# The heads' norms: squares summed in two f32r products in place of one fp32 product

## The chip, the cores and the metric

One core of a Trainium2 chip runs the whole kernel in one launch. TensorE (PE; its weight loads are shown as PEld), VectorE (DVE), ScalarE (ACT) and GpSimd (POOL) each work through a queue of their own in order, and wait for each other through semaphores; transfers are issued by SyncE (SP) and by POOL. The metric is the device time in microseconds (us) of one execution. Before the change it is 901.6 us, the median of three runs that lie between 899.93 and 905.34 us.

## The reference

One layer of a hybrid transformer on 528 tokens (16 meta tokens and 512 others) of width 1024, in fp32. Three kinds of attention run on the same normed input: stick-breaking heads (`sb`, 4 heads), sparse heads that see the 132 best keys by an indexer (`sp`, 4 heads), and differential heads (`df`, 4 heads, two maps each). Each has a gate and an output projection; then come `w_out`, a residual, and a gated feed-forward net with a short convolution. What the change touches is the norm over the channels of a head:

```python
def _rmsnorm(a, gain):
    af = a.astype(jnp.float32)
    af = af * lax.rsqrt(jnp.mean(af * af, axis=-1, keepdims=True) + EPS)
    return (af * gain.astype(jnp.float32)).astype(a.dtype)
...
    _indexed_sparse_attention(_rmsnorm(hd(q_sp, SP_HEADS), q_norm_sp),
                              _rmsnorm(hd(k_sp, SP_HEADS), k_norm_sp), ...)
    q_df = _rmsnorm(q_df.reshape(b, tp, DF_HEADS, 2, HEAD_DIM), q_norm_df)
    k_df = _rmsnorm(k_df.reshape(b, tp, DF_HEADS, 2, HEAD_DIM), k_norm_df)
    ...
    y_df = _rmsnorm(y_df, subln_df) * (1.0 - lam_init)
```

## The kernel before

Activations stand with channels on the 128 partitions and tokens along the row, so 128 channels (two heads of 64) of 528 tokens are one tile. Each dense product is made of three f32r products: an fp32 number is split into a rounded f32r part (`xh`, `wh`) and what is left (`xl`, `wl`), and hi*hi + lo*hi + hi*lo is summed in PSUM (`mm3`). A dense chunk of 128 outputs takes two halves of the tokens (258 and 256 columns, or 264 twice), and each half 24 products of TensorE into a bank `psd`; DVE then multiplies the bank by the row norm `rs` into SBUF. These last steps are the evacuations.

The work from 100 us on follows a list, `PLAN`: units (`sb0`, `df0`, ..., `sp1`: a q, a k and a v chunk each), gate chunks (`g0a`, ...) and branch projections (`b0a`, ...). The piece of the list that matters here is `... df3 g2b sp0 sp1 b2a b2b g1a g1b b1a b1b`. Beside this main line run streams, Python generators that are advanced one step after every eight dense products (`tick`): for each unit one for q, k and v (norm, split, moves between partitions), one for the scores and weights, one for the products with the values, and for `df` one for the output `y`. The top-132 search of the indexer (`topk_stream`) is another stream: 17 rounds of `max` and `match_replace` on DVE over four blocks of queries, one round per `PACE` of the planner's clock. The `sp` scores wait until it is finished (`picked`).

When a stream goes on is decided while the program is built, by booked costs: every DVE, ACT and POOL instruction adds a cost to a clock of its engine (`book`), every product to PE's (`pe`; `mm` books an fp32 product of n columns at 2*0.844*n ns and an f32r product at 0.46*n+1 ns), and `settle` holds a stream until PE's clock has passed what it waits for. So a change of costs moves other instructions as well. A branch cannot start before the outputs of its units are booked as done (`until`): `b2a` needs `y` of all four `df` units, and its TensorE instructions stand behind them in PE's queue.

`headnorm` is the step that is changed. It is used for q and k of `sp0`, `sp1` and `df0` to `df3` (12 norms, constant `blk`: two blocks of 64x64 with -0.5/64) and for the output of `df0` to `df3` (4 norms, constant `ones2` with -0.5/128). ACT squares the tile, TensorE multiplies the square with the constant in two halves, which leaves in every partition the sum over the head's channels, and `rstd` makes 1/sqrt of it (Ln, Exp, Square on ACT, two steps on DVE). 16 norms of two halves are 32 products; a product of fp32 operands shows in the trace as two MATMUL records with two weight loads. In the trace `ones2` is called `ones`, and all instructions of the three vector engines have line 99, that of the booking helper.

Of the kernel before, what the change touches and what calls it, by code (L numbers as in the profile page):

```python
# [8 lines left out]
F32 = mybir.dt.float32  # L9
F32R = mybir.dt.float32r  # L10
AF = mybir.ActivationFunctionType
OP = mybir.AluOpType
# [3 lines left out]
P = 128  # L16
# [39 lines left out]
def tile_kernel(ctx: ExitStack, tc, hT, wpk, par, bias, yT):  # L56
# [25 lines left out]
    class Timed:  # L82
# [11 lines left out]
        def __getattr__(self, op):  # L94
            f = getattr(self.eng, op)

            def run(out, *a, **k):
# [5 lines left out]
    V = Timed("V", nc.vector, 1.04, 150, scalar_tensor_tensor=(1.25, 105), tensor_tensor_scan=(2.16, 110),  # L103
              tensor_tensor_reduce=(1.0, 255), match_replace=(1.04, 220))
    S = Timed("S", nc.scalar, 0.84, 190)
# [18 lines left out]
    def pe(cost):  # L124
        c = cur[0]
        ready = c["t"] if c["t"] != c.get("pe") and c is not main else 0
        clock["P"] = max(clock["P"], ready) + cost
        c["t"] = c["pe"] = clock["P"] + LAT


    const = ctx.enter_context(tc.tile_pool(name="const", bufs=1))
# [12 lines left out]
    def bank(tag):  # L144

        while sum(h["t"] + BSL > clock["P"] for h in held[tag]) >= banks[tag]:
            yield
        h = {"t": math.inf}
        held[tag].append(h)
        return ps.tile([P, 512], F32, tag=tag, bufs=banks[tag], name="ps" + tag), h  # L150

    def drop(h):
        h["t"] = cur[0]["t"]
# [9 lines left out]
    def give(tag, n=1):  # L163
        free[tag] += n
        assert free[tag] <= caps[tag], tag
# [5 lines left out]
    def wait(tag, n=1):  # L171
        while free[tag] < n:
            yield
        take(tag, n)

    def tmp(dt=F32):
        return ap_.tile([P, T], dt, tag="tmp", bufs=caps["tmp"], name="tmp")

    def mm(out, lhsT, rhs, **k):

        n, w = rhs.shape[-1], 0.84 * max(32, lhsT.shape[-1])
        pe(max(0.46 * n + 1, w) if rhs.dtype == F32R else 2 * max(0.844 * n, w))
        PE.matmul(out, lhsT, rhs, **k)  # L183
# [38 lines left out]
    def settle(more=0):  # L222

        c = cur[0]
        while clock["P"] < c["t"] + more + SLACK:
            yield
# [23 lines left out]
    make_identity(nc, ident)  # L250
    onesd = const.tile([P, P], F32, name="onesd")
    V.memset(onesd, -0.5 / D)
    ones2 = const.tile([P, P], F32, name="ones2")
    V.memset(ones2, -0.5 / 128)
    blk = const.tile([P, P], F32, name="blk")
    V.memset(blk, 0.0)
    V.memset(blk[0:64, 0:64], -0.5 / 64)
    V.memset(blk[64:128, 64:128], -0.5 / 64)
    eps = const.tile([P, 1], F32, name="eps")
    V.memset(eps, EPS)  # L260
    one = const.tile([P, 1], F32, name="one")
# [18 lines left out]
    for w in plan:  # L280
# [5 lines left out]
        else:  # L286
            n = BRW[br] // 2
# [97 lines left out]
    def wbank():  # L385
        return ps.tile([P, 512], F32, tag="w", bufs=banks["w"], name="psw")
# [21 lines left out]
    ixd, st = [wbank(), wbank()], [wbank(), wbank()]  # L408
# [16 lines left out]
    def rstd(dst, st, y0, a, now=True):  # L425

        S.activation(dst, st, AF.Ln, bias=eps, scale=-2.0)
        S.activation(y0, dst, AF.Exp, scale=-0.5)
        S.activation(a, y0, AF.Square)
        rstd2(dst, st, y0, a) if now else None  # L430

    def rstd2(dst, st, y0, a):
        V.scalar_tensor_tensor(a, st, -0.5 * EPS, a, OP.add, OP.mult)
        V.scalar_tensor_tensor(dst, a, 1.5, y0, OP.add, OP.mult)

    y0, a0 = tmp(), tmp()
# [199 lines left out]
    def headnorm(raw, n, gain, mat):  # L636

        yield from wait("tmp", 4)
        sq, r, y0, a = tmp(), tmp(), tmp(), tmp()
        S.activation(sq[:, :n], raw[:, :n], AF.Square)  # L640
        yield from settle()
        for o, w in (HALQ if n == TQ else HALF):
            t0 = cur[0]["t"]
            st, b = yield from bank("w")
            cur[0]["t"] = 0
            mm(st[:, :w], mat, sq[:, o:o + w], start=True, stop=True)
            x = r[:, o:o + w], st[:, :w], y0[:, o:o + w], a[:, o:o + w]
            rstd(*x, now=False)
            yield from settle(-SET)
            rstd2(*x)  # L650
            drop(b)
            yield
        V.scalar_tensor_tensor(raw[:, :n], raw[:, :n], gain, r[:, :n], OP.mult, OP.mult)
        give("tmp", 4)
# [7 lines left out]
    def q_stream(unit, raw, gain):  # L662


        n = TQ
        if gain is not None:
            yield from headnorm(raw, n, gain, blk)
        yield from wait("qk", 2)
        yield from wait("tmp")
        a, b, l = qtile(), qtile(), tmp(F32R)  # L670
        S.copy(a[:, :n], raw[:, :n])
        sub(l[:, :n], raw[:, :n], a[:, :n])
        move(b[64:128, :n], a[64:128, :n])
        move(b[0:64, :n], l[64:128, :n])
        move(a[64:128, :n], l[0:64, :n])
        give("tmp", 2)
        unit["q"] = (a, b)
        unit["t"] = max(unit.get("t", 0), cur[0]["t"] + 6500)

    def k_stream(unit, raw, gain):  # L680


        n = T
        if gain is not None:
            yield from headnorm(raw, n, gain, blk)
        yield from wait("qk", 4)
        a, b, l, m = qtile(), qtile(), qtile(), qtile()
        S.copy(a, raw)
        sub(l, raw, a)
        for x, y in ((a, b), (l, m)):  # L690
            move(y[64:128], x[64:128])
            move(y[0:64], x[64:128])
            move(x[64:128], x[0:64])
        give("tmp")
        unit["k"] = (a, b, l, m)
        unit["t"] = max(unit.get("t", 0), cur[0]["t"] + 6500)
# [286 lines left out]
    def y_stream(unit, paired):  # L983
        yr = unit["yr"]
        if not paired:
            yield from headnorm(yr, TQ, gsub, ones2)
        yield from wait("y", 2)
        yh, yl = (ap_.tile([P, TQ], F32R, tag="y", bufs=caps["y"], name="y") for _ in range(2))
        S.copy(yh, yr[:, :TQ])
        sub(yl, yr[:, :TQ], yh)  # L990
        give("tmp")
        unit["y"] = (yh, yl)
        unit["done"] = cur[0]["t"]
# [92 lines left out]
    for m in range(8):  # L1086
        a = gates[0, m // 4][:, m % 4]
# [12 lines left out]
    def ft(dt=F32):  # L1100
        return ffn.tile([P, TQ], dt, tag="ft", bufs=10, name="ft")

    for m in range(8):
# [18 lines left out]
        sq = ss if m == 0 else ft()  # L1122
# [36 lines left out]
    for f in range(NF):  # L1159
# [11 lines left out]
        a = ft()  # L1171
# [9 lines left out]
    for m in range(8):  # L1181
# [3 lines left out]
        for c in sorted({e // 8 for e in range(e0, e1)}):  # L1185
# [5 lines left out]
                start=es[0] == e0, stop=es[-1] == e1 - 1)  # L1191
# [77 lines left out]
```

## Time and profile before

| | us |
|---|---|
| median of three runs | 901.6 |
| the profiled execution | 906.82 |
| its span on the core | 904.7 |
| PE busy in the span | 869.8 |
| DVE busy | 534.1 |
| ACT busy | 453.6 |
| POOL busy | 248.9 |

The span is the time from the first to the last instruction of the core in the trace, and the 2.1 us around it are launch and end. A share of the whole span is an average over stages: the start to about 100 us, the attention with its dense chunks to about 360 us, the branches and the last units to about 480 us, and the output projection and the feed-forward net to the end. Rows of a timeline give the start (us from the span's start), the duration, the engine, the line, the operation, the tiles out<-in and the count of merged instructions.

### The profile page before, as it was taken

To read this page: it belongs to the slowest core of one execution; us is meant where nothing else is said; L and a number is where in the kernel's file an instruction comes from. 1 tells how busy PE (TensorE), PEld (TensorE's weight loads), DVE (VectorE), ACT (ScalarE), POOL (GpSimd) and SP (SyncE) were. 2 spreads that over 40 slices of the span, in tenths; PEclk is the share of its full clock that TensorE was granted. 3 is DMA by queue.
4 is the path that set the end of the run, shared out by engine and by line. 5 is a ranking of instruction groups with operands and counts; after the bars stand their busy time and mean duration, and the time that the engine had idled before them with its cause. 6 is when DMAs were issued, how large, how long until landed. Compare 5 with 4: busy or idle time off the path is not lost.

```text
span 904.7 us, 15408 instructions
## 1 busy us (share of the span) xinstructions
PE 869.8 (96%) x6066; PEld 808.5 (89%) x6066; DVE 534.1 (59%) x1145; ACT 453.6 (50%) x848; POOL 248.9 (28%) x200
## 2 busy tenths in 40 slices
PE   6898999999999999699998999999999999999998
PEld 6897999999999999698998999999999999888886
DVE  6559969888778787777446444455444444322221
ACT  6446877787757777554663353333333333211110
POOL 2335012131113112564043234444434444200100
PEclk9899999999999999899999999999999999999999
DMA  6576635574557644643554323323333233333330
GB/s 210 161 199 195 159 92 132 136 164 107 111 126 174 153 116 113 146 97 81 130 117 161 95 76 93 93 93 94 93 96 92 93 94 96 97 118 110 117 108 29
DMA packets 35959, 107.79 MB, mean 119 GB/s; under 512 B 4713, under 2 KB 4857, under 8 KB 35888
## 3 DMA queue, kind: packets, MB, share of 16 engines
q1 hardware_dynamic: 27968, 78.19, 28.9%
q0 software_dynamic: 7920, 28.64, 15.0%
q8 instruction: 47, 0.77, 0.4%
q14 instruction: 24, 0.20, 0.1%
HBM read 93.99 MB, written 5.86 MB: 110 GB/s over the span
## 4 chain that ended last, share of the span: by engine, by line
PE 76%; DVE 10%; ACT 4%; DMA 4%; POOL 2%; issue 2%; SPq 0%; ACTq 0%; POOLq 0%; DVEq 0%
PE psd L183 53%; PE psw L183 21%; DVE tmp L99 4%; ACT tmp L99 2%; PE psw L187 2%; DMA wr<-wpk 2%; DMA qk<-qk 1%; DVE work L99 1%; DVE G L99 1%; ACT wl L99 1%; POOL tmp L99 1%; DVE wl L99 1%; DMA wh<-wpk 1%; DVE m L99 1%; DMA wl<-wpk 1%
## 5 line engine op out<-in xcount | busy, mean ns | idle before, releaser
L99 ACT CAST wh<-wr 128x1024 fp32r<-128x1024 f32 (+2 forms) x112 | 114.2, 1021 | 219.3 <-DMA wr<-wpk 171.9
L99 DVE TENSOR_TENSOR wl<-wr,wh 128x1024 fp32r<-128x1024 f32 (+2 forms) x80 | 93.2, 1166 | 70.1 <-PE psd L183 67.9
L99 POOL TENSOR_TENSOR wl<-wr,wh 128x1024 fp32r<-128x1024 f32 x32 | 81.1, 2537 | 180.1 <-PE psd L183 95.0
L183 PE MATMUL psd<-xh,wh 128*128 128x258 f32 (+2 forms) x792 | 119.5, 290 | 5.1 <-DVE tmp L99 3.5
L183 PE MATMUL psd<-xh,wl 128*128 128x258 f32 (+2 forms) x792 | 117.0, 288 | 1.1 <-POOL wl L99 1.1
L183 PE MATMUL psd<-xl,wh 128*128 128x258 f32 (+2 forms) x792 | 117.7, 289 | 0.0
L183 PEld LDWEIGHTS psd<-xh,wh 128*128 128x128 f32 x792 | 105.0, 191 | 6.9 <-issue 3.6
L183 PEld LDWEIGHTS psd<-xh,wl 128*128 128x128 f32 x792 | 104.1, 191 | 2.1 <-POOL wl L99 1.3
L183 PEld LDWEIGHTS psd<-xl,wh 128*128 128x128 f32 x792 | 104.4, 190 | 0.7
L99 ACT ACTIVATE tmp<-tmp 128x528 f32<-128x528 f32 (+7 forms) x154 | 69.0, 475 | 15.8 <-DVE tmp L99 13.4
L99 POOL TENSOR_TENSOR ft<-ft 128x512 f32<-128x512 f32 x22 | 46.8, 2127 | 84.0 <-DVE ft L99 84.0
L99 DVE SCALAR_TENSOR_TENSOR ft<-ft,prm 128x512 f32<-128x512 f32 x44 | 48.3, 1097 | 29.3 <-ACT ft L99 28.5
L334 POOL DMA_DIRECT2D wl<-wpk x25 | 22.1, 885 | 120.2 <-ACT wl L99 94.2
L183 PE MATMUL psw<-uh,wh 128*128 128x256 f32 (+2 forms) x264 | 47.0, 320 | 0.0
L183 PE MATMUL psd<-uh,wh 128*128 128x258 f32 (+2 forms) x264 | 46.9, 319 | 0.0
L183 PE MATMUL psd<-uh,wl 128*128 128x258 f32 (+2 forms) x264 | 46.9, 319 | 0.0
L183 PE MATMUL psw<-ul,wh 128*128 128x256 f32 (+2 forms) x264 | 46.8, 319 | 0.0
L183 PE MATMUL psw<-uh,wl 128*128 128x256 f32 (+2 forms) x264 | 46.8, 319 | 0.0
L183 PE MATMUL psd<-ul,wh 128*128 128x258 f32 (+2 forms) x264 | 46.8, 319 | 0.0
L183 PE MATMUL psd<-al,wh 128*128 128x512 f32 x176 | 45.8, 396 | 0.0
L183 PE MATMUL psd<-ah,wl 128*128 128x512 f32 x176 | 45.8, 396 | 0.0
L183 PE MATMUL psd<-ah,wh 128*128 128x512 f32 x176 | 45.8, 396 | 0.0
(196 smaller groups left out, 1672.9 us busy)
## 6 DMA issues: line engine op xcount, KB each, us to landing
wr<-wpk SPq DMA_DIRECT2D x106, 512.0 KB, 3.6
wh<-wpk POOLq DMA_DIRECT2D x25, 512.0 KB, 4.0
wl<-wpk POOLq DMA_DIRECT2D x25, 512.0 KB, 5.7
qk<-qk SPq DMA_DIRECT2D x48, 132.0 KB, 2.9
gd<-tab SPq DMA_DIRECT2D x8, 328.0 KB, 5.6
tmp<-hT SPq DMA_DIRECT2D x8, 264.0 KB, 6.8
W<-gd POOLq DMA_DIRECT2D x8, 264.0 KB, 3.9
qk<-tmp SPq DMA_DIRECT2D x16, 128.5 KB, 3.7
```

The source lines that it names most:

```text
L99: return f(out, *a, **k)
L183: PE.matmul(out, lhsT, rhs, **k)
L187: PE.transpose(out, x, ident[:x.shape[0], :x.shape[0]])
L334: nc.gpsimd.dma_start(wl, chunk(a), accum_op=OP.add)
```

## The change

The constants `blk` and `ones2` become f32r (both are exact powers of two). `headnorm` squares the tile twice on ACT, into the fp32 tile `sq` and into the f32r tile `sh`, subtracts one from the other on DVE into the f32r tile `sl`, and multiplies both parts with the constant, two f32r products into the same bank. `r` and `a` now share the memory of `sq`, so that the step still takes four tiles of the pool.

```diff
-    ones2 = const.tile([P, P], F32, name="ones2")
-    V.memset(ones2, -0.5 / 128)
-    blk = const.tile([P, P], F32, name="blk")
+    ones2 = const.tile([P, P], F32R, name="ones2")
+    V.memset(ones2.bitcast(F32), -0.5 / 128)
+    blk = const.tile([P, P], F32R, name="blk")
...
         yield from wait("tmp", 4)
-        sq, r, y0, a = tmp(), tmp(), tmp(), tmp()
+        sq, sh, sl, y0 = tmp(), tmp(F32R), tmp(F32R), tmp()
         S.activation(sq[:, :n], raw[:, :n], AF.Square)
+        S.activation(sh[:, :n], raw[:, :n], AF.Square)
+        V.tensor_tensor(sl[:, :n], sq[:, :n], sh[:, :n], OP.subtract)
+        r, a = sq, sq
         yield from settle()
...
-            mm(st[:, :w], mat, sq[:, o:o + w], start=True, stop=True)
+            mm(st[:, :w], mat, sh[:, o:o + w], start=True, stop=False)
+            mm(st[:, :w], mat, sl[:, o:o + w], start=False, stop=True)
```

Since the booked costs change, the streams take their turns elsewhere. Two places follow.

PE before, from the last dense half of `sp1` (its v chunk, `wh_4757`) to the first product with all four `df` outputs. `psd<-y` x3 are products of `b2a` with the first three outputs; `ones_81` is the norm of the output of `df3`, the two `blk` rows of 264 columns are the norm of `sp1`'s k, the rows with `ident` transpose `sp1`'s v, `qk` are scores of `sp0`:

```order
L183 MATMUL psd<-xh,wl_4758 128x264 x8
L183 MATMUL psd<-y,wh_4969 128x258 x3
L183 MATMUL psd<-y,wh_4969 128x256 x3
L183 MATMUL psd<-y,wh_4969 128x258 x3
L183 MATMUL psw<-tmp,ones_81 128x258
L183 MATMUL psw<-tmp,blk 128x264
L183 MATMUL psw<-tmp,ones_81 128x256
L187 MATMUL psw<-ident,tmp 128x128 x4
...
L183 MATMUL psw<-qk 128x144
L183 MATMUL psw<-qk 128x272
L183 MATMUL psd<-y,wh_4969 128x258 x5
```

PE now, the same stretch (the v chunk is `wh_4761`, `pt` and `pm` are weights of `df3` that are multiplied with its values, the first `ones_81` rows are the norm of `df2`'s output, the last ones that of `df3`):

```order
L183 MATMUL psd<-xh,wl_4762 128x264 x8
L183 MATMUL psw<-tmp,ones_81 128x258 x2
L187 MATMUL psw<-ident,tmp 16x128 x2
L187 MATMUL psw<-ident,tmp 128x128 x7
L183 MATMUL psw<-tmp,ones_81 128x256 x2
...
L183 MATMUL psw<-pm_463,vm 128x256
L183 MATMUL psw<-pt,vt 128x256 x9
L183 MATMUL psw<-pt,vt 128x128 x3
L183 MATMUL psw<-tmp,blk 128x258 x2
...
L183 MATMUL psw<-qk 128x400 x2
L183 MATMUL psd<-y,wh_4964 128x258 x5
```

The norms of `df2`'s output and of `sp1`'s q (two products each before) and the last 9 transposes and 13 value products of `df3` have moved from among the dense halves to behind the last of them, and 15 score products of `sp0` (3 before) with two transposes stand ahead of the first product with all four outputs.

DVE before, from the evacuation of that last dense half. The rows on `work` are the last round of the search; the row with `gsub` ends the norm of `df3`'s output, 19 instructions after the evacuation:

```order
L99 TENSOR_TENSOR tmp<-psd,rs 128x264
L99 MATCH_REPLACE work_443<-m_5041,work_443 128x404
L99 SCALAR_TENSOR_TENSOR tmp<-tmp 128x264
L99 TENSOR_SCALAR work_442<-work_442 128x272
...
L99 MATCH_REPLACE work_444<-m_5098,work_444 128x532
...
L99 TENSOR_TENSOR vt<-psw,vt 128x8x64
...
L99 SCALAR_TENSOR_TENSOR tmp<-psw,tmp 128x264
L99 SCALAR_TENSOR_TENSOR tmp<-tmp,gsub 128x514
```

DVE now, the same stretch; `tmp<-tmp 128x514` and `128x528` without a constant are the new subtractions, and the row with `gsub` at the end is again that of `df3`, 52 instructions after the evacuation:

```order
L99 TENSOR_TENSOR tmp<-psd,rs 128x264
L99 TENSOR_TENSOR pm_463<-psw,pm_463 16x256
L99 SCALAR_TENSOR_TENSOR tmp<-psw,tmp 128x258
L99 TENSOR_TENSOR pt<-psw,pt 128x512
...
L99 TENSOR_TENSOR tmp<-tmp 128x514
L99 MAX m_5079<-work_444 128x8
L99 SCALAR_TENSOR_TENSOR tmp<-tmp,gsub 128x514
...
L99 TENSOR_TENSOR tmp<-tmp 128x528
L99 MAX m_5119<-work_442 128x8
...
L99 SCALAR_TENSOR_TENSOR tmp<-tmp,gsub 128x514
```

Behind the last evacuation there is now nearly a whole further round of the search, three subtractions, and the DVE part of the steps that moved on PE.

## Rows read from the trace of the kernel before

**Rows 1.** The page: busy time by engine, and the span in 40 slices (tenths).

```profile
PE 869.8 (96%) x6066; PEld 808.5 (89%) x6066; DVE 534.1 (59%) x1145; ACT 453.6 (50%) x848; POOL 248.9 (28%) x200
PE   6898999999999999699998999999999999999998
DVE  6559969888778787777446444455444444322221
```

**Rows 2.** Windows: the stretch and its length, then busy us (instructions) by engine.

```profile
100.00:360.00 260.00, 257.35 (x2096) 252.31 (x2095) 207.68 (x558) 194.48 (x412) 47.84 (x58) 1.00 0.55 129
360.00:373.00 13.00, 4.67 (x25) 3.25 (x24) 11.49 (x25) 9.95 (x23) 5.18 (x5) 0.87 0.63 134
373.00:413.00 40.00, 38.88 (x309) 37.75 (x308) 30.23 (x94) 17.04 (x47) 29.96 (x30) 0.96 0.48 107
```

**Rows 3.** Waits of PE, longest in total: us, times, longest.

```profile
PE psw L183 <- DMA qk<-qk: 5.1, 1, 5.1
PE psw L183 <- ACT tmp L99: 4.3, 3, 2.3
```

**Rows 4.** Timeline of PE, two norm products among dense products.

```profile
351.19 0.60 PE L183 MATMUL psw<-tmp,blk 128*128 128x258 f32 x2
351.43 1.33 PE L183 MATMUL psd<-xh,wl 128*128 128x264 f32 x8
352.61 0.61 PE L183 MATMUL psw<-tmp,blk 128*128 128x264 f32 x2
352.85 1.33 PE L183 MATMUL psd<-xh,wh 128*128 128x264 f32 x8
354.03 1.14 PE L183 MATMUL psd<-xl,wh 128*128 128x264 f32 x8
355.00 0.59 PE L183 MATMUL psw<-tmp,blk 128*128 128x256 f32 x2
```

**Rows 5.** The norm's products and their weight loads: count of records, busy, mean ns.

```profile
L183 PEld LDWEIGHTS psw<-tmp,blk x48: 186/188/193, 132.4 to 366.8; 128*128 128x128 f32 x48
L183 PE MATMUL psw<-tmp,blk 128*128 128x264 f32 x24 | 7.7, 402 | 1.9 <-DVE tmp L99 1.5 <-ACT tmp L99 0.5
L183 PE MATMUL psw<-tmp,ones 128*128 128x258 f32 x8 | 2.5, 394 | 2.3 <-ACT tmp L99 2.3
```

**Rows 6.** Groups of DVE and ACT by form: count, busy us, mean ns.

```profile
L99 DVE TENSOR_TENSOR tmp<-tmp 128x528 f32<-128x528 f32 x11 | 8.7, 791 | 0.2
L99 DVE TENSOR_TENSOR y<-tmp,y 128x514 fp32r<-128x514 f32 x1 | 0.7, 695 | 0.1
L99 DVE SCALAR_TENSOR_TENSOR tmp<-tmp,gsub 128x514 f32<-128x514 f32 x4 | 3.0, 743 | 0.0
L99 DVE SCALAR_TENSOR_TENSOR tmp<-psw,tmp 128x258 f32<-128x258 f32 x10 | 4.2, 422 | 1.9 <-ACT tmp L99 1.8
L99 DVE MAX8 m<-work 128x8 f32<-128x532 f32 x17 | 12.0, 706 | 0.0
L99 ACT ACTIVATE tmp<-tmp 128x528 f32<-128x528 f32 x30 | 18.2, 636 | 8.1 <-DVE tmp L99 7.7 <-DVE xl L99 0.2
```

**Rows 7.** Timeline, from the last dense evacuation to the branch's products.

```profile
360.06 0.43 DVE L99 TENSOR_TENSOR tmp<-psd,rs 128x264 f32<-128x264 f32 x1
...
362.81 2.18 DVE L99 TENSOR_SCALAR work<-work 128x400 f32<-128x400 f32 x1
...
365.85 0.43 DVE L99 TENSOR_SCALAR work<-work 128x528 f32<-128x528 f32 x1
...
370.29 0.75 DVE L99 SCALAR_TENSOR_TENSOR tmp<-tmp,gsub 128x514 f32<-128x514 f32 x1
...
371.07 0.62 ACT L99 CAST y<-tmp 128x514 fp32r<-128x514 f32 x1 [1.16 <-DVE tmp L99]
...
372.44 0.82 PE L183 MATMUL psw<-qk 128*2 128x16 f32 x3 [5.05 <-DMA qk<-qk]
...
373.06 1.28 PE L183 MATMUL psd<-y,wh 128*128 128x258 f32 x5
```

More of the change, by code (lines that the diff above doesn't have):

```diff
@@ L252, in tile_kernel @@
     V.memset(onesd, -0.5 / D)
-    ones2 = const.tile([P, P], F32, name="ones2")
-    V.memset(ones2, -0.5 / 128)
-    blk = const.tile([P, P], F32, name="blk")
-    V.memset(blk, 0.0)
-    V.memset(blk[0:64, 0:64], -0.5 / 64)
-    V.memset(blk[64:128, 64:128], -0.5 / 64)
+    ones2 = const.tile([P, P], F32R, name="ones2")
+    V.memset(ones2.bitcast(F32), -0.5 / 128)
+    blk = const.tile([P, P], F32R, name="blk")
+    V.memset(blk.bitcast(F32), 0.0)
+    V.memset(blk.bitcast(F32)[0:64, 0:64], -0.5 / 64)
+    V.memset(blk.bitcast(F32)[64:128, 64:128], -0.5 / 64)
     eps = const.tile([P, 1], F32, name="eps")
```

## The prediction

> **What bounds the kernel now.** I read the page first: PE is busy for 96% of the span, DVE for 59% and ACT for 50%, but by slices DVE stands at 7 to 9 tenths in the attention, while PE has dips at the start, in the 17th slice and in the 22nd [rows 1]. So I looked at windows. From 100 to 360 us, where nearly all of the norms lie, PE is busy 257.35 of 260.00 us, DVE 207.68 (80%) and ACT 194.48 (75%) [rows 2]: that stretch is bound by PE, and work taken off PE shortens it as long as DVE and ACT keep up. From 360 to 373 us it is the other way round: PE is busy 4.67 of 13.00 us, DVE 11.49 and ACT 9.95 [rows 2]. PE's longest single waits are there, 5.1 us for a move of `qk` and 2.3 us for ACT [rows 3]. From 373 on PE is busy again, 38.88 of 40.00 us [rows 2]. So the kernel is a long stretch bound by PE, a short one bound by the chain through DVE and ACT, and PE again. The short one begins when the last dense half of `sp1` has been evacuated, at 360.06 us, and ends when `b2a` can multiply with all four `df` outputs, at 373.06 us [rows 7]; from then on PE has filling work.
>
> **What the change takes off PE.** A norm product of 264 columns delays what follows it by 0.45 us: from the one at 352.61 to the dense group at 354.03 are 1.42 us, and the eight dense products in between take 0.97 us by themselves (354.03 to 355.00) [rows 4]. The product of 256 columns or 258 comes to about 0.43, so I use 0.44. A dense f32r product of 264 columns takes 0.97/8 = 0.121 us [rows 4], so the two f32r products that come in its place take 0.24. That is 0.20 us saved for each of 32 products, 6.4 us on PE. The "busy" of the group, 402 ns for a record [rows 5], would give more; durations of neighbouring records overlap, so I take the distance of starts.
>
> **What it adds.** 16 squares on ACT: 0.636 us each for 528 columns [rows 6], 10.1 us. 16 subtractions on DVE: two fp32 operands in SBUF and f32r out, between 0.695 (the only row of that kind and nearly that size) and 0.791 us (two-operand steps early in the kernel) [rows 6]; I take 0.74, 11.8 us. In the stretch bound by PE (13 of the 16) both go into idle time: DVE had 52 us of it and ACT 65 [rows 2]. The price there is nothing as long as evacuations aren't late; the order supports it, since DVE has 665 instructions up to the last dense evacuation against 670 before, although 13 subtractions were added: other work has been pushed behind it. Behind it is no cover: that is the short stretch, where DVE is busy for 88%. The norm's product now also waits for DVE behind ACT; queued behind it on PE are dense products, which is harmless where its data are early and not where PE has nothing else.
>
> **The sum goes by three places.** First, the end of the dense halves. Before it stood 28 of the 32 products (28 x 0.44 = 12.3 us), now 24 pairs (24 x 0.24 = 5.8 us): 6.5 us less. And 9 transposes and 13 value products of `df3` have moved behind; at some 0.10 us each (an estimate, under the 0.121 of a product of 264 columns, since many are narrower) 2.2 us. So the last evacuation comes 8.7 us earlier, at about 351.4 instead of 360.06.
>
> Second, the stretch from there to `b2a`. Before, 19 DVE instructions lead from the evacuation to the `gsub` step of `df3`'s norm: 8 norm steps on 256 to 264 columns at 0.42, two on 514 and 528 at 0.74, three search steps (0.57, 0.71 and 0.70, with 0.16 for loading values), three marks on `work` at 0.43, and 1.0 for `vt` and `vm`, together 9.3 us [rows 6, 7], the narrower search step scaled by its width. In the trace they take from 360.49 (360.06 + 0.43) to 371.04 (370.29 + 0.75), 10.55 us [rows 7]; the difference is one mark that took 2.18 us. Now there are 52: 16 norm steps at 0.42 (6.7), four at 0.74 (3.0), three subtractions at 0.74 (2.2), four `max` and four `match_replace` (5.2), three marks (1.3), five steps for `pm`, `pt`, `vt` and `vm` (2.6, at 0.42 to 0.70) and 13 small ones (1.8): 22.8 us. With as much loss as before, 1.25 us or 13%, this is 24.0 to 25.8, and I take 24.9. The cast of `y` on ACT adds 0.62 and the start of PE 0.1. So the stretch takes 25.6 us, where from 360.49 to 373.06 it took 12.57: 13.0 us more. The move of `qk` that PE waited 5.1 us for no longer decides: the norm of `sp0`'s k stands nine dense groups ahead of the end now, three before. What is late next is `y` of `df3`.
>
> Third, what PE has left from `b2a` on is less by 12 score products and 2 transposes that it has done while waiting: 14 x 0.10 = 1.4 us.
>
> Together -8.7 + 13.0 - 1.4 = **+2.9 us**. The profiled execution took 906.82 us, so it would take 909.7; against the median of 901.6 it is **904.5 us**. What the norms give back on PE is lost, and a little more, while PE waits at the end of the dense halves.
>
> The bounds: if DVE runs its 52 instructions without a gap, the stretch is 22.8 + 0.7 = 23.5, 10.9 more than before, and the sum +0.8. If four norms in a row each leave one more square and one more hand-over uncovered (about 1 us each), it is +7.
>
> **The rivals.** (1) PE's saving arrives whole, and PE waits as long as before: -6.4 us, 895.2 us. For it speaks that PE is busy for 99% from 100 to 360 us; against it that the DVE queue fixes the order, and nothing of those 52 instructions can start before the evacuation ahead of them. Chance 0.12.
>
> (2) Slower by over 1%: in the late stretch ACT and DVE take turns instead of overlapping. A norm there goes ACT twice, DVE, PE, ACT three times, DVE twice, and four of them (`df2` and `df3` outputs, q and k of `sp1`) stand behind the dense end, with no dense product to hide a hand-over. DVE was busy for 88% of the old stretch; at 70% the 22.8 us would take 32.6 and the sum would be -8.7 + (33.3 - 12.6) - 1.4 = +10.6 us, 912.2 us. It is over the 1% mark (9 us) from a share of 0.73 down. Against it: four norms are more to overlap, not less, and the search fills gaps. Chance 0.10.
>
> (3) The products don't get cheaper, because PE is held by weight loads: the norm has two records and two loads for each fp32 product, 48 loads of 188 ns for `blk` [rows 5], and will have as many with two f32r products. Then 6.5 us drop out of the first place, and the sum is -2.2 + 13.0 - 1.4 = +9.4 us, 911 us. Against it: dense products have a load each and still start 0.121 us apart, where the fp32 pair needs 0.44 with the same two loads [rows 4, 5]. Chance 0.03. The Trainium skill has a rule that points this way (Perfetto Trace Analysis, Identifying the Most-Contended Engine): the busy time of matmuls is no good measure of how close PE is to its limit, and the busy share of LDWEIGHTS is to be used. By that measure the change would free nothing; the rows just named don't bear it out for these products.
>
> **How the numbers follow.** About 1% (9 us) is what a measurement of this kernel can tell from no change; its three runs spread over 0.6%. Forecast, between -2 and +7 us: 0.72. Rivals: 0.12, 0.10 and 0.03; 0.03 are left for orders elsewhere that turn out well or badly. All of the forecast and rival 1 lie within 1%, so that is 0.81; slower by over 1% has rivals 2 and 3 and the upper edge, 0.15; faster by over 1% would need the short stretch to shrink although 33 instructions were added to it, 0.04. The range is 895 to 911 us: from rival 1 to the upper bound of the stretch with the spread of the runs.
>
> **What would show it.** Right: norm products as 64 single records, a pair some 0.24 us apart from what follows; the last dense evacuation near 351 us; PE mostly idle for some 25 us from there, with DVE busy for about 90%, and the clock granted to PE lower there, as it was from 360 to 373 us (0.87 [rows 2]); the first product with four outputs at 376 to 379 us; everything from `b1a` on as before. Wrong: if that product comes before 372 us, rival 1 or something near it is right; after 384 us, rival 2; if the dense end doesn't come earlier than 356 us, the products or DVE's load in the stretch ahead were misjudged.

## The result, and the profile after

The changed kernel takes 908.2 us (median of 9 runs, 904.59 to 911.34) where the kernel before, run beside it, took 902.0 us (9 runs, 899.93 to 905.64): a ratio of 1.0053, 95% interval [1.0034, 1.0072], that is some 4.8 us slower. Forecast were +2.9 us (904.5), with a range of 895 to 911. The profiled execution took 909.64 us, with a span of 907.9.

The page of the changed kernel (busy time by engine, then slices in tenths) answers to [rows 1]:

```profile
PE 868.2 (96%) x6066; PEld 806.1 (89%) x6066; DVE 540.9 (60%) x1161; ACT 458.4 (50%) x864; POOL 249.3 (27%) x200
PE   7898999999999998699998999999999999999998
DVE  6659968968778789986446544444444444322221
```

PE is busy for only 1.6 us less, not 6.4, and its dip before the middle (a 6 in the 17th slice) is still there. DVE has gained 6.8 us of work and stands at 9 in the 16th and 17th.

The groups by form show both sides of the change (count, busy us, mean ns, then idle time ahead), where [rows 5, 6] have the old ones:

```profile
L183 PE MATMUL psw<-tmp,blk 128*128 128x264 f32 x24 | 5.4, 300 | 0.4 <-DVE m L99 0.4
L99 DVE TENSOR_TENSOR tmp<-tmp 128x514 fp32r<-128x514 f32 x10 | 7.3, 731 | 0.0
L99 DVE TENSOR_TENSOR tmp<-tmp 128x528 fp32r<-128x528 f32 x6 | 4.4, 730 | 1.8 <-ACT tmp L99 1.8
L99 ACT ACTIVATE tmp<-tmp 128x514 fp32r<-128x514 f32 x10 | 6.2, 621 | 0.0
L99 ACT ACTIVATE tmp<-tmp 128x528 fp32r<-128x528 f32 x6 | 3.8, 636 | 0.0
```

The subtractions take 0.73 us each, 11.7 in all (forecast 0.74, 11.8), the added squares 10.0 (forecast 10.1).

PE's longest waits in total (us, times, longest), against [rows 3]:

```profile
PE psw L183 <- ACT tmp L99: 7.8, 3, 6.1
...
PE psw L183 <- DVE pm L99: 2.8, 3, 1.4
...
PE psw L183 <- DMA qk<-qk: 2.2, 3, 1.1
```

The wait of 5.1 us for the move of `qk` has gone; one of 6.1 us for ACT has come, for the squares of `df3`'s output norm. The three short waits for `qk` stand at 214 and 291 us, where PE did not wait for it before.

The timeline of the changed kernel, PE, DVE and POOL together, from two norm products among dense ones to the branch; it answers to [rows 4, 7]:

```profile
343.43 0.40 PE L183 MATMUL psw<-tmp,blk 128*128 128x264 f32 x2
343.68 1.13 PE L183 MATMUL psd<-xh,wh 128*128 128x264 f32 x8
344.64 1.14 PE L183 MATMUL psd<-xl,wh 128*128 128x264 f32 x8
...
350.06 1.57 POOL L99 TENSOR_TENSOR qk<-tmp,qk 128x528 fp32r<-128x528 f32 x1 [3.14 <-ACT qk L99]
...
350.35 1.84 DVE L99 SCALAR_TENSOR_TENSOR tmp<-tmp,r 128x528 f32<-128x528 f32 x1
...
351.93 1.13 PE L183 MATMUL psd<-xh,wl 128*128 128x264 f32 x8
...
354.52 0.42 DVE L99 TENSOR_TENSOR tmp<-psd,rs 128x264 f32<-128x264 f32 x1
...
364.00 0.42 DVE L99 SCALAR_TENSOR_TENSOR tmp<-tmp 128x258 f32<-128x258 f32 x1
364.33 0.30 DVE L99 TENSOR_SCALAR work<-work 128x272 f32<-128x272 f32 x1
...
369.99 0.80 PE L183 MATMUL psw<-tmp,ones 128*128 128x258 f32 x2 [6.10 <-ACT tmp L99]
...
375.71 0.73 DVE L99 SCALAR_TENSOR_TENSOR tmp<-tmp,gsub 128x514 f32<-128x514 f32 x1
...
378.04 1.28 PE L183 MATMUL psd<-y,wh 128*128 128x258 f32 x5
```

A pair of f32r products puts off what follows by 0.25 us (343.43 to 343.68), the fp32 product by 0.45. The last dense product ends at about 352.9 (0.97 us for eight, from 351.93), but the evacuation stands in DVE's queue until 354.52, 1.6 us; in the kernel before it came 0.3 us behind PE's end (360.06 behind 359.75). From there to the first product of `b2a` with all four outputs are 23.5 us (354.52 to 378.04), before 13.0 [rows 7].

Two executions can't be compared by the clock time of their rows alone: the thirteenth evacuation of a dense half, behind the same instructions in the same order, begins between 75.4 and 81.8 us in the fourteen profiles of this study. So I count from it (**A**), and take as further marks the last dense half but two ahead of the late stretch (**B**; two more evacuations follow it) and the fourteenth evacuation of a half behind that stretch (**C**). Windows of the kernel before between these marks (stretch, length, then busy us and instructions of PE, PEld, DVE, ACT, POOL, the granted clock, DMA share, GB/s):

```profile
81.14:352.80 271.66, 267.77 (x2182) 262.03 (x2182) 218.19 (x587) 204.73 (x442) 50.41 (x61) 1.00 0.58 138
352.80:458.66 105.86, 95.42 (x765) 92.28 (x764) 71.68 (x192) 57.78 (x122) 42.85 (x44) 0.97 0.49 112
```

and of the changed kernel, first by the marks, then the late stretch by itself and what follows:

```profile
80.70:348.20 267.50, 261.26 (x2171) 257.09 (x2171) 216.38 (x587) 205.01 (x445) 48.96 (x60) 1.00 0.59 139
348.20:461.60 113.40, 100.12 (x778) 95.17 (x777) 79.87 (x211) 62.27 (x135) 44.08 (x44) 0.92 0.46 107
...
352.00:376.00 24.00, 13.18 (x73) 10.07 (x71) 22.03 (x65) 19.57 (x51) 8.42 (x9) 0.76 0.48 107
376.00:413.00 37.00, 35.22 (x272) 34.27 (x273) 30.93 (x89) 15.70 (x40) 23.85 (x23) 0.93 0.36 89
```

From A to B the changed kernel is 4.2 us faster, from B to C 7.5 us slower. From A to C it needs 380.9 us instead of 377.5: PE's busy time falls by 1.8 (363.2 to 361.4), and its idle time grows by 5.2 (14.3 to 19.5). If the products save 6.4, the other work of PE has become 4.6 us dearer, and the granted clock between B and C points to where: 0.92 instead of 0.97.

### The profile page after: what moved, and what is told of

It reads as the page before. It is cut to its first block, busy times and chain, and to the rows that moved or that the text cites. A ratio compares the mean times of both kernels' runs of the same rounds, so it can differ in the third digit from the quotient of the medians.

```text
span 907.9 us, 15462 instructions
## 1 busy us (share of the span) xinstructions
PE 868.2 (96%) x6066; PEld 806.1 (89%) x6066; DVE 540.9 (60%) x1161; ACT 458.4 (50%) x864; POOL 249.3 (27%) x200
## 4 chain that ended last, share of the span: by engine, by line
PE 65%; DVE 11%; ACT 8%; DMA 7%; issue 5%; POOL 3%; SPq 0%; ACTq 0%; POOLq 0%; DVEq 0%
PE psd L183 45%; PE psw L183 19%; DVE tmp L99 5%; ACT tmp L99 3%; DMA qk<-qk 3%; DMA wl<-wpk 1%; DVE work L99 1%; PE psw L187 1%; DVE G L99 1%; ACT wl L99 1%; POOL tmp L99 1%; ACT G L99 1%; DMA wr<-wpk 1%; DVE wl L99 1%; DVE m L99 1%
## 5 line engine op out<-in xcount | busy, mean ns | idle before, releaser
L99 ACT ACTIVATE tmp<-tmp 128x528 f32<-128x528 f32 (+9 forms) x170 | 76.7, 489 | 18.9 <-DVE tmp L99 15.3
L335 POOL DMA_DIRECT2D wl<-wpk x25 | 22.2, 886 | 134.4 <-ACT wl L99 113.4
```

What stands on the lines that cost most here:

```text
L99: return f(out, *a, **k)
L335: nc.gpsimd.dma_start(wl, chunk(a), accum_op=OP.add)
```

## The experiments

All were timed in five rounds beside the kernel before. The last column is worked out from the ratio (times 902 us); A to B and so on are from windows as above, of one profile each.

| kernel | A to B | B to C | A to C, against before | ratio, 95% interval | us against before |
|---|---|---|---|---|---|
| before | 271.7 | 105.9 | 377.5 | | |
| the change | 267.5 | 113.4 | +3.4 | 1.0053 [1.0034, 1.0072] | +4.8 |
| e1_books | 271.7 | 107.4 | +1.6 | 1.0014 [0.9998, 1.0030] | +1.3 |
| e2b_added | 273.2 | 104.5 | +0.1 | 0.9989 [0.9966, 1.0012] | -1.0 |
| e2c_order | 275.1 | 108.3 | +5.9 | 1.0043 [1.0023, 1.0064] | +3.9 |
| e3b_products | 268.2 | 107.3 | -2.0 | 0.9980 [0.9957, 1.0004] | -1.8 |
| f1_single | 267.8 | 106.8 | -3.0 | 0.9976 [0.9952, 0.9999] | -2.2 |
| f2_warm_after | 272.1 | 113.6 | +8.2 | 1.0085 [1.0056, 1.0114] | +7.7 |
| f3_warm_books | 271.4 | 107.8 | +1.7 | 1.0060 [1.0038, 1.0083] | +5.4 |
| f4_warm_before | 271.2 | 105.3 | -1.1 | 1.0005 [0.9985, 1.0024] | +0.5 |
| g1_dve | 272.0 | 106.1 | +0.6 | 0.9996 [0.9977, 1.0015] | -0.4 |
| g3_pool | 274.0 | 108.1 | +4.6 | 1.0056 [1.0031, 1.0082] | +5.1 |
| f1_dve | 267.9 | 105.2 | -4.4 | 0.9952 [0.9928, 0.9975] | -4.3 |
| b_dve | 271.8 | 106.0 | +0.3 | 0.9995 [0.9972, 1.0018] | -0.5 |

But for f3_warm_books, the profile's A to C and the measured difference agree within some 2 us, so the windows can be used to say where a difference lies. Kernels that run the same instructions from A to B mostly agree there within 0.6 us (271.2 to 271.8 for the kernel before, f4_warm_before and b_dve; 271.4 to 272.0 for e1_books, f3_warm_books and g1_dve). The exception is the changed kernel: f2_warm_after runs the same instructions up to B and takes 272.1 us, 4.6 more.

**The parts of the change.** The change does three things at once: cheaper products, added work on ACT and DVE, and another order, since the planner books what is issued. The first four kernels take these apart.

e1_books: all instructions of the change, in nearly the order of before.

```diff
-        S.activation(sh[:, :n], raw[:, :n], AF.Square)
-        V.tensor_tensor(sl[:, :n], sq[:, :n], sh[:, :n], OP.subtract)
+        nc.scalar.activation(sh[:, :n], raw[:, :n], AF.Square)
+        nc.vector.tensor_tensor(sl[:, :n], sq[:, :n], sh[:, :n], OP.subtract)
...
-            mm(st[:, :w], mat, sh[:, o:o + w], start=True, stop=False)
-            mm(st[:, :w], mat, sl[:, o:o + w], start=False, stop=True)
+            pe(2 * 0.844 * w)
+            PE.matmul(st[:, :w], mat, sh[:, o:o + w], start=True, stop=False)
+            PE.matmul(st[:, :w], mat, sl[:, o:o + w], start=False, stop=True)
```

> All instructions of the change, but booked as the kernel before booked its norm, so that the streams take their turns as before (4 norm products of 2 halves behind the last dense half instead of 8, 20 DVE steps from there to the last output norm instead of 52). Theory of the prediction (products save 6.4 us on PE, the loss comes from steps that moved behind the dense halves): about 5 us faster than before, 895 to 899 us, the three subtractions and squares in the late stretch costing 1 to 2 us. Rival (the added squares and subtractions themselves eat the gain, wherever the steps stand): within 2 us of the changed kernel, 905 to 909 us. Rival (the products save nothing): 903 to 905 us.

Measured: 902.9 us, by the ratios 3.5 us better than the change, but not under the kernel before and not the 895 to 899 of the theory. B to C is back to 107.4 from 113.4; A to B is no shorter than before, although the 26 products that stand ahead of B in this order are 0.20 us cheaper each.

e2b_added: the kernel before with the second square and the subtraction, neither of them used.

```diff
         S.activation(sq[:, :n], raw[:, :n], AF.Square)
+        nc.scalar.activation(a[:, :n], raw[:, :n], AF.Square)
+        nc.vector.tensor_tensor(y0[:, :n], sq[:, :n], a[:, :n], OP.subtract)
         yield from settle()
```

> The kernel before, with the second square and the subtraction added and not booked; the fp32 product stays and reads neither. Order as before. Theory: the added work goes into idle time of ACT and DVE and costs 0.5 to 2 us, 902.5 to 904 us. Rival (added work is the cause): 8 us or more, 910 us and up.

Measured: no difference in the time. In its profile A to B is 1.5 us longer and B to C 1.4 shorter.

e2c_order: the instructions of before, with the bookings of the change.

```diff
         S.activation(sq[:, :n], raw[:, :n], AF.Square)
+        book("S", S.cost(a[:, :n], "activation"))
+        book("V", V.cost(y0[:, :n], "tensor_tensor"))
...
-            mm(st[:, :w], mat, sq[:, o:o + w], start=True, stop=True)
+            pe(0.46 * w + 1)
+            pe(0.46 * w + 1)
+            PE.matmul(st[:, :w], mat, sq[:, o:o + w], start=True, stop=True)
```

> The instructions of the kernel before (one square, one fp32 product), with the costs of the change booked, so that the streams take their turns nearly as in the changed kernel. Theory: the late stretch grows as in the changed kernel without the gain on the products: 8 to 12 us slower than before, 910 to 914 us, with the first product of all four outputs some 20 us behind the last dense evacuation. Rival (order costs nothing): 902 us.

Measured: 3.9 us slower than before, without any of the added work. The first product with all four outputs comes 22.7 us behind the last dense evacuation (359.21 to 381.91; 13.0 before, 23.5 in the changed kernel). PE's longest wait behind 350 us is the one of the changed kernel, to a tenth (L650 is the norm's product there):

```profile
PE psw L650 <- ACT tmp L99: 6.2, 1, 6.2
```

So the order by itself makes most of the loss. It is smaller than the 8 to 12 us that I had put down for it, and not all of it arises behind the dense halves: in this profile 3.4 of the 5.9 us lie from A to B. PE waits there for a move of `qk`, and the next dense groups of eight start 1.72 us apart, where they took 0.95 ahead of it; the granted clock is 0.72 from 212 to 224 us:

```profile
215.74 1.25 PE L183 MATMUL psw<-qk 128*2 128x16 f32 x5 [3.33 <-DMA qk<-qk]
216.79 1.92 PE L183 MATMUL psd<-xh,wh 128*128 128x258 f32 x8
```

The three profiles in the new order all have waits for `qk` from A to B (3.3 us here, 2.2 in the changed kernel, 3.0 in f2_warm_after); the eleven in the old order have none.

e3b_products: two f32r products, the second with a matrix of zeros; the low part of the squares and its subtraction are left out.

```diff
-        S.activation(sq[:, :n], raw[:, :n], AF.Square)
+        S.activation(sh[:, :n], raw[:, :n], AF.Square)
...
-            mm(st[:, :w], mat, sq[:, o:o + w], start=True, stop=True)
+            pe(2 * 0.844 * w)
+            PE.matmul(st[:, :w], mat, sh[:, o:o + w], start=True, stop=False)
+            PE.matmul(st[:, :w], zmat, sh[:, o:o + w], start=False, stop=True)
```

> Two f32r products, but the low part of the squares is left out: one f32r square on ACT, no subtraction, and the second product has a constant of zeros. Booked as before. Theory: the gain of the products alone, 5 to 6.4 us faster than before, 895.5 to 897 us. Rival (weight loads hold PE, the products save nothing): within 1 us of before.

Measured: 1.8 us faster, at the edge of the noise, and less than a third of the 6.4 us that the products save. From A to B 3.4 arrive of some 5.2 (26 products); from B to C 1.4 are lost again. Against it, e1_books with its squares and subtractions takes 3.5 us longer from A to B: that is the price of the added work in the stretch that I had called free. PE waits there 1.5 us in all for the subtractions themselves.

f1_single: one product, on squares rounded to f32r; the low part is left out here, too.

```diff
-            PE.matmul(st[:, :w], mat, sh[:, o:o + w], start=True, stop=False)
-            PE.matmul(st[:, :w], zmat, sh[:, o:o + w], start=False, stop=True)
+            PE.matmul(st[:, :w], mat, sh[:, o:o + w], start=True, stop=True)
```

> One f32r product for each half of a norm, on squares rounded to f32r; the low part, its subtraction and its product are left out, and the planner books what it booked before, so that the order is that of the kernel before. TensorE has 32 x 0.32 = 10.2 us less to do (0.44 for the fp32 product, about 0.12 for one f32r product), where the pair with the zero matrix had 6.4 less and came out 1.8 us faster. Theory (new waits ahead of the last dense evacuation take about 1.5 us, and the late stretch takes back as much again, because TensorE comes to it earlier and then idles and runs at the lower clock): 4 to 5 us faster than before, 896.5 to 898, the last dense evacuation 6 to 7 us earlier than before counted from the same early evacuation. Rival 1 (TensorE's work arrives whole, and the pair lost its gain to something of its own): 10 us faster, 891. Rival 2 (VectorE and ScalarE set the time once TensorE has any slack, so that no more arrives than with the pair): 1 to 2 us faster, about 900.

Measured: 2.2 us faster than before. Of 3.8 us more that are taken off PE, 0.4 (by the ratios, within their noise) to 1.0 (by the profiles) arrive. Rival 2 was nearest: A to B doesn't shrink any more (267.8 against 268.2), PE's idle time takes it (7.2 us of A to B, against 5.2 in e3b_products and 3.9 before).

**The lower clock.** In the late stretch PE idles and then runs at 0.50, 1.2 GHz: from about 370 to 376 us before, from 364 to 381 in the changed kernel, from 359 to 375 in e1_books. I thought that the missing gain was there, and put idle products (no part of the computation) into the waits.

```diff
+            if mat is ones2 and o == 0:
+                calls["ones"] += 1
+                for _ in range(20 if calls["ones"] == 4 else 0):
+                    PE.matmul(st, xh[:, 0, :P], xh[:, 1, :512], start=True, stop=True)
```

f2_warm_after has 20 of them in the changed kernel, f3_warm_books 14 in e1_books, at the same place, and f4_warm_before 14 in the kernel before, ahead of the first scores of `sp0`.

> The changed kernel with 20 idle products of 512 columns (about 0.21 us each, 4.3 us; their result is overwritten and is no part of the computation) put on TensorE ahead of the first product of the last subtraction norm, that is into its wait of 6.1 us at 364 to 370 us. Theory (the lower clock behind that wait is part of the loss: in the changed kernel TensorE runs at 0.50 from about 364 to 381 us, and is busy for some 3 us of that after the first product of b2a and in some products on the chain ahead of it): the granted clock stays at 1.00 through the stretch and the kernel is 2 to 3.5 us faster than the changed kernel, 905 to 906. Rival (the chain of VectorE and ScalarE sets the stretch and the clock costs nothing): 908, with the clock at 1.00 all the same. A clock that falls nevertheless leaves both open.

> The kernel with all instructions of the change in about the order of before (e1_books, 902.9 us), with 14 idle products of 512 columns (about 3.0 us, no part of the computation) put on TensorE right behind the last dense product, into the wait of 4.45 us there. All other instructions keep their order. Theory (the gain of the cheaper products is lost to the lower clock: in e1_books TensorE runs at 0.50 from about 358.6 to 375.2 us and is busy for some 6 us of it behind the first product of b2a): 3 to 4 us faster than e1_books, 899 to 900, which is under the time before by 1.5 to 2.5 us; the granted clock at 1.00 through the stretch. Rival (the stretch is set by VectorE's and ScalarE's chain and by the transfers, the clock costs nothing): 902 to 903.

> The kernel before with 14 idle products of 512 columns (about 3.0 us, no part of the computation) put on TensorE ahead of the first scores that wait 5.05 us for a transfer at 367 to 372 us. Theory (there, too, the lower clock behind the wait costs, but less: 0.50 from about 369.7 to 376.2, TensorE busy for 3.8 us of it): about 1.9 us faster than before, 899.5 to 900. Rival (the clock costs nothing): 901.5. With this run the share of the clock in the difference between the kernels is told apart: by the theory the three kernels with idle products differ by what the cheaper products and the added waits are worth alone.

Measured: none of the three got the gain back. f3_warm_books is 4 us slower than e1_books, f4_warm_before equal to before; f2_warm_after came out 3 us above the changed kernel, with intervals that overlap. The idle products don't account for that: from B to C it takes 113.6 us, the changed kernel 113.4, and the difference of the two profiles lies from A to B, ahead of them. What f2_warm_after can't test is the clock, as its windows and the idle products themselves show:

```profile
362.00:369.00 7.00, 6.80 (x19) 5.53 (x20) 6.93 (x22) 5.07 (x15) 1.30 (x1) 0.53 0.00 1
369.00:375.00 6.00, 4.10 (x26) 3.12 (x24) 5.58 (x20) 5.04 (x16) 5.74 (x6) 1.00 0.56 125
375.00:382.00 7.00, 6.45 (x29) 5.62 (x29) 6.58 (x22) 3.06 (x12) 4.43 (x6) 0.53 0.30 68
```

The clock had fallen before they began at 363.98, they took 6.88 us instead of 4.3, and the clock fell once more where `b2a` begins. In f3_warm_books they ran at 1.00 (14 in 3.37 us), but the granted clock then stood at 0.50 from about 367 to 381 us, and `b2a` began at it; that is no test either. The clean case is f4_warm_before, in windows:

```profile
359.00:363.00 4.00, 2.28 (x18) 1.95 (x16) 4.00 (x12) 3.12 (x5) 1.57 (x2) 1.00 0.08 16
363.00:367.00 4.00, 3.36 (x9) 2.69 (x10) 3.88 (x8) 3.15 (x8) 2.37 (x3) 0.57 1.00 175
367.00:375.00 8.00, 6.43 (x37) 4.84 (x36) 4.73 (x11) 4.81 (x13) 2.48 (x2) 1.00 0.55 133
```

`b2a` begins at 1.00 there, and A to C is 1.1 us shorter than before; in the time nothing of it can be seen. So the lower clock at the start of `b2a` is worth about 1 us in the kernel before. What it is worth in the changed kernel stays open. Open, too, is why f3_warm_books takes 907.9 us: from A to C its profile has 379.2 us, as e1_books has, but A itself lies at 80.4 instead of 75.9; its six runs (905.05 to 910.25) all stand above the median of e1_books.

**A meeting of DVE and POOL.** The late stretch of e1_books has one DVE row that is three times as long as its like. Its timeline from the last dense evacuation on:

```profile
354.48 0.43 DVE L99 TENSOR_TENSOR tmp<-psd,rs 128x264 f32<-128x264 f32 x1
...
355.92 2.35 DVE L99 SCALAR_TENSOR_TENSOR tmp<-tmp,prm 128x528 f32<-128x528 f32 x1
...
356.14 1.55 POOL L99 TENSOR_TENSOR tmp<-tmp,qk 128x514 fp32r<-128x514 f32 x1
...
360.04 0.58 PE L651 MATMUL psw<-tmp,ones 128*128 128x258 f32 x1 [4.45 <-ACT tmp L642]
```

The gain product of the keys (`prm`) ends 0.58 us after POOL's subtraction, as if it had stood still until then; the cast of the keys, and behind it on ACT the squares that PE waits for, come after it. e3b_products has the same row with 2.42 us. In the kernel before, the product had passed earlier, and the row of 2.18 us [rows 7] was a mask of the search. g1_dve moves that one subtraction from POOL to DVE.

```diff
         S.copy(a[:, :n], raw[:, :n])
-        sub(l[:, :n], raw[:, :n], a[:, :n])
+        if unit is byname.get(("sp", 1)):
+            book("G", G.cost(l[:, :n]))
+            nc.vector.tensor_tensor(l[:, :n], raw[:, :n], a[:, :n], OP.subtract)
+        else:
+            sub(l[:, :n], raw[:, :n], a[:, :n])
```

> All instructions of the change in about the order of before (e1_books), and one subtraction more moved: the low part of the last queries (128 x 514), which GpSimd made at 356.1 to 357.7 us there, is made by VectorE ahead of the gain product of the keys; booked as before, so that the order stays. Theory (the gain product took 2.35 us there instead of the 0.77 of the kernel before because it ran into that instruction of GpSimd, and the squares of the last norms wait for it): the subtraction takes 0.73 and the gain product 0.75 to 0.8, the product ends 0.9 us earlier than in e1_books, counted from the last dense evacuation, and the first product with ones comes 4.6 to 4.8 us behind that evacuation instead of 5.56; in the time that is about 0.9 us, less than the measurement tells (902 +- 1). Rival (the 2.35 us are of another cause, say the operands or a transfer): the gain product takes 2.3 us again and the first product with ones comes 6 us or more behind the evacuation; 903 to 904.

Its timeline, the same place (L680 is the subtraction that was moved):

```profile
354.56 0.42 DVE L99 TENSOR_TENSOR tmp<-psd,rs 128x264 f32<-128x264 f32 x1
...
356.01 0.68 DVE L680 TENSOR_TENSOR tmp<-tmp,qk 128x514 fp32r<-128x514 f32 x1
356.61 0.76 DVE L99 SCALAR_TENSOR_TENSOR tmp<-tmp,prm 128x528 f32<-128x528 f32 x1
...
356.92 0.39 PE L651 MATMUL psw<-tmp,ones 128*128 128x258 f32 x1 [1.24 <-ACT tmp L642]
```

The gain product takes 0.76 us, the product with ones comes 2.36 us behind the evacuation instead of 5.56 (4.6 to 4.8 expected), and B to C is 1.3 us shorter. The time follows by about as much (0.9996 against 1.0014), which is at the edge of what five rounds tell. The Trainium skill has the rule (SBUF — State Buffer, SBUF: two separate sides): VectorE and GpSimd share a pair of ports to SBUF, an instruction of VectorE with two inputs in SBUF or in a two-port mode needs it, and whoever comes second stands still for the whole of the other's instruction. The rows agree that the two hinder each other: 2.35 us with POOL's instruction beside it, 0.76 without. Which came first they don't show: DVE's row begins 0.22 us before POOL's.

f1_dve is the same edit on f1_single (low part of the squares left out), b_dve on the kernel before.

> One f32r product for each half of a norm on squares rounded to f32r (f1_single; the low part is left out), with the low part of the last queries made by VectorE instead of GpSimd, as in g1_dve. In f1_single a mask of the search (1.88 us instead of 0.30) stood behind that instruction of GpSimd, and the gain product of the keys behind the mask. Theory (that meeting costs the late stretch about 1.6 us less the 0.73 of the subtraction): 0.9 us faster than f1_single, 1.0040 to 1.0030 times faster than before, that is some 899.5 where before has 902.5, and the mask at 0.30. Rival (the late stretch ends on a transfer or on ScalarE anyway): no change, 900.5.

> The kernel before with the low part of the last queries made by VectorE instead of GpSimd. There a mask of the search, which no one on the chain waits for at once, took 2.18 us instead of 0.35 beside GpSimd's two low parts; the gain product of the keys had passed before them. Theory (the meeting costs before less than it costs the kernels with cheaper products): the time stays within 0.5 us, 902, since the subtraction adds 0.73 on VectorE ahead of the gain product and the mask gives back up to 1.8 behind it. Rival (the mask is on the chain, too): 1 us faster. If g1_dve gains and this one doesn't, the late 1.6 us of the kernels with cheaper products are shown to be this meeting.

Measured: f1_dve is 4.3 us faster than before, 2.1 more than f1_single, with B to C 1.6 us shorter: twice what I expected, and the best time of all kernels here (898.2 us beside 901.8). That f1_dve beats the kernel before is clear of the noise, that it beats f1_single is not (their intervals overlap); there the windows carry the reading. b_dve is level with before. So, by the windows, the meeting costs nothing in the order and at the pace of before and about 1.5 us once PE gets to the late stretch earlier.

g3_pool puts the 16 subtractions of e1_books on POOL, which has time.

```diff
-        nc.vector.tensor_tensor(sl[:, :n], sq[:, :n], sh[:, :n], OP.subtract)
+        nc.gpsimd.tensor_tensor(sl[:, :n], sq[:, :n], sh[:, :n], OP.subtract)
```

> All instructions of the change in about the order of before (e1_books), with the 16 subtractions of the low part on GpSimd in place of VectorE, booked as before. VectorE has 11.8 us less to do, GpSimd about 16 x 1.3 = 21 us more. Theory 1 (what the added work costs ahead of the last dense evacuation, 3.4 us from the same early evacuation against the kernel without squares and subtraction, is VectorE's load): that stretch comes 2 to 3 us shorter; the late stretch grows by 0.6 us for each of two subtractions on its chain, and the time is 901 to 902. Theory 2 (GpSimd's instructions stop VectorE's while both run, as at the gain product of 2.35 us): VectorE gains nothing, its two-input instructions that meet a subtraction take 1 to 2 us more each, and the time is 904 to 906.

Measured: 907.5 us beside 901.8, nearer to theory 2 (904 to 906) than to theory 1, but by another way. Ahead of 355 us PE waits for the subtractions themselves (L652 is the second product of a pair):

```profile
PE psw L652 <- POOL tmp L643: 4.3, 6, 1.7
```

A to B grows by 2.3 us over e1_books. In e1_books the same waits, for DVE, come to 1.5 us in 4. So the longer way of the data, and not DVE's load, goes with the loss there; whether DVE was stopped by POOL as well was not looked at row by row.

## Why the prediction held, and where not

The total was right, +2.9 us forecast and +4.8 measured; in the profile, from A to C, +3.4. That it came so near is in part luck: in the profile the first place is short by 3.6 us and the second too large by 2.5, and the two errors cancel. The three places of the sum, counted from A:

| place | forecast | profile |
|---|---|---|
| last dense evacuation | -8.7 | -5.1 (354.52 - 80.70 against 360.06 - 81.14) |
| from there to the first product with four outputs | +13.0 | +10.5 (23.5 against 13.0) |
| from there on, to C | -1.4 | -2.0 (83.6 against 85.6) |

**The price of a product** was right: 0.25 us for a pair, 0.24 forecast. Rival 3 falls with it: the 48 weight loads are there as before (`PEld` x6066 in both pages), and the delay fell all the same. The rule of the Trainium skill on LDWEIGHTS that the prediction named beside it isn't borne out for these products.

**"The price there is nothing"** is the step that failed: the stretch bound by PE was taken to lose nothing, neither to the added work nor to the new order. The last evacuation came 3.6 us later than forecast. The profile has 2.3 us of it as idle time of PE from A to B (3.9 to 6.2 us), and 1.3 as the evacuation's longer wait in DVE's queue (1.6 instead of 0.3 us), ahead of which stands the row of 1.84 us that ran beside POOL's at 350.06. Of that idle time 2.2 us are the waits for `qk`, which e2c_order has without any added work, so they go with the order; none is a wait for a subtraction. What the added work costs is shown in the old order, by e1_books against e3b_products: 3.5 us. The size in the changed kernel rests on one profile: in f2_warm_after, with the same instructions, the last evacuation comes 278.4 us behind A, only 0.5 earlier than before. How the loss divides between order and added work there stays open. That DVE had 52 us of idle time there [rows 2] doesn't make an instruction free that stands ahead of an evacuation or in the middle of a norm.

**The late stretch** went as described: idle PE, DVE at 92% (22.03 of 24 us), a product with four outputs at 378.04 (376 to 379 forecast). Its size was 2.5 us too large, and the term that was mis-sized is the loss between DVE instructions: the rows of the 52 add up to some 22.7 us, as forecast (22.8), but take 21.5 (354.94 to 376.44), since neighbouring rows overlap (364.00 + 0.42 against 364.33). The 1.25 us of loss that I scaled up came from one mark of 2.18 us beside POOL [rows 7]. Its cause was half told: I counted 33 more DVE instructions, added and moved ones alike. e2c_order has only the moved ones and its stretch grows by 9.7 us (13.0 to 22.7), nearly as in the changed kernel; e2b_added has only the added ones and no loss. So the stretch grows because the norm of `df3` and the search stand behind the dense end, and that was the planner's answer to the new bookings.

**Rival 1** (the saving arrives whole) isn't true even where order and added work are taken out: of 6.4 us 1.8 arrive. What is taken off PE ahead of the dense end goes partly into small waits there (PE's idle time from A to B grows by 1.3 us in e3b_products) and brings PE earlier to a place where it waits anyway. **Rival 2** (taking turns, DVE at 70%) falls by DVE's 92%.

Better than both kernels is f1_dve, on squares rounded to f32r: a single product, none of the added work, and one instruction out of POOL's way.

## What to carry to other kernels

Where a planner or scheduler makes the order from costs, run the new costs with the old instructions and the new instructions with the old costs: here the order alone was worth some 4 us and the instructions some 1, each within about 2. A saving on the bounding engine is worth what its next wait leaves of it; price the wait at the end of the stretch before the saving. And when one row of DVE is two or three times as long as its like, look at POOL in the same microseconds.

## What was not expected of the hardware

A VectorE row with two inputs in SBUF (0.76 us) took 2.35, and masks with one input took 2.18 and 1.88 instead of 0.30 to 0.35, each beside a GpSimd instruction on SBUF. TensorE's clock fell to 0.50 in the late stretch of every kernel, at different places (354 to 371 us), and in f2_warm_after 20 products in a row ran at it. The first 80 us of the program took 75.4 to 81.8 us from one execution to the next, more than most of the differences that were looked for; which is why all of them are counted from a common row. The rows tell two kinds apart: in eight profiles PE waits 3.5 us for DVE at about 30 us, the granted clock from 28 to 42 us is 0.76 to 0.88, and A lies at 79.5 to 81.8; in the other six the wait is 1.0 to 1.2, the clock 1.00, and A lies at 75.4 to 76.1. Why the wait differs no run shows.
